# A seven-product feed-forward stage: raw weights of every other tile in slots of their own, the sums and the last block formed earlier, low parts of the down weights on VectorE

## The chip, the cores and the metric

The kernel runs on one NeuronCore of a Trainium2 chip. The metric is the device time of one execution in microseconds: 2243.45 us, the median of three runs (2242.74 to 2244.39). Five engines run their own instruction streams in order: TensorE (PE, matrix products), VectorE (DVE), ScalarE (ACT), GpSimd (POOL) and SyncE (SP, which here issues the transfers). They wait for one another only through semaphores.

## The reference

One step of a small decoder trunk, in fp32, for a prompt of 1024 + 16 tokens and 8 sample sequences of 4 tokens, model width 1024, two layers. Every layer adds a mixer (layer 0: a state-space model beside a short convolution; layer 1: a Conformer convolution module) and then a feed-forward part of hidden width 2816, 22 tiles of 128 columns:

```python
def conv_ffn(xn, fbuf, p, l):
    u = xn @ p['w_ffn_up'][l]
    a, g = jnp.split(u, [D_FF], axis=-1)
    a_c, nbuf = causal_dwconv(a, fbuf, p['w_ffn_conv'][l])
    return (jax.nn.silu(a_c) * g) @ p['w_ffn_down'][l], nbuf
```

So for each hidden tile there are two up products (a and g), a causal depthwise convolution of width 3 over a, silu, a product with g, and the down product, which is added to the residual. At the end stands a final rmsnorm.

## The kernel before

Tokens are worked on in two parts (hf = 0 and 1), and every stage runs part by part. To keep fp32 accuracy every matrix is split into a high and a low part, and a product of two matrices is three matmuls: high by high, low by high, high by low. For a weight block that means a transfer into `raw`, ScalarE's copy to the high part (`wh`) and a subtraction (`wl = raw - wh`).

The change touches the last stage alone: layer 1, tokens of part 1 (560 columns), `f1.run(1, "v", None, finals, out0)`. Its up products use a Strassen-like scheme, `up7`: the two weight blocks of a hidden tile (128x1024 each, a and g) are cut in halves a11, a12, a21, a22 of 128x512. From them come the sums s1 = a21 + a22, s2 = s1 - a11, s4 = a12 - s2 and s3 = a11 - a21, and seven products of 280 columns take the place of eight: w11, ws1, w12, ws2, ws4, ws3 and a22. Each is 12 matmuls, so a tile is 84. In between, VectorE and ScalarE move results from the accumulators (`bx`, `by`, `bz`) into `ap` and `g`, form the convolution `c` (ScalarE starts it, two VectorE operations end it), then silu into `s`, `s` times `g`, and the split of `s` into `hh` and `hl`, the operands of the down product. The a22 product is held back (`self.pend`) and issued in the next tile or in the down (`flush`); its result goes into `s` by one more VectorE operation.

The 22 tiles run in groups: f0 and f1, then four at a time (f2 to f5, ..., f18 to f21). After the up tiles of a group comes its down product, 8 output blocks of 24 matmuls for each tile of 128x1024 `w_down`; the first up tile of the next group is issued ahead of it. So f2 is issued before the down of f0 and f1, and f3 is the first up tile after it; f6 comes before the down of f2 to f5 and f7 after it, and so on with f10 and f14; the last group is issued whole ahead of the down of f14 to f17.

The order of instructions on each engine is the work of a scheduler, which moves instructions from their place in the program by its own estimates of when inputs are ready; what it makes of it is fixed when the kernel is built. The raw weights have two buffers of 4 KB per partition ("raw", `bufs=2`) in a ring: a transfer waits until the block that was there has been read by all of its users, and transfers that SP issues later wait behind it. In `up7`, a11 and a12 are the one block and a21 and a22 the other. `slot(tag, ...)` takes a slot from pools that other stages have used ("v", "xh", "t", "x"). `weight()` loads the down weights through the same ring; its low part is formed by POOL or VectorE by a counter (`WPOOL`), if no engine is given. `L1167` scales a block of the first part's final output, `L1168` sends it off; these run as fill-in work during the stage. In the changed program all lines from L869 on are some 7 higher (L870 is L877, L897 is L904, L1167 is L1174).

Of the kernel before, what the change touches and what calls it, by code (L numbers as in the profile page):

```python
# [12 lines left out]
F32 = mybir.dt.float32  # L13
F32R = mybir.dt.float32r
# [7 lines left out]
P = 128  # L22
# [15 lines left out]
FT = FF // P  # L38
# [13 lines left out]
MUL, ADD, SUB = ALU.mult, ALU.add, ALU.subtract  # L52
# [12 lines left out]
GROUPS = grp(0, 2, 2) + grp(2, FT, 4)  # L65


def build(nc, tc, ctx, a):
# [8 lines left out]
    def slot(tag, name, shape, dt=F32):  # L77
        if isinstance(shape, int):
            shape = [P, TN[shape]]
        n = math.prod(shape[1:])  # L80
        assert n <= SW
        t = sl.tile([P, SW], dt, tag=tag, name=name, bufs=COUNT[tag])
        v = t[:shape[0], :n]
        if len(shape) > 2:
            n = " ".join(f"d{i}" for i in range(len(shape) - 1))
            v = v.rearrange(f"p ({n}) -> p {n}", **{f"d{i}": shape[i + 1] for i in range(len(shape) - 2)})
        return v
# [12 lines left out]
    def tt(o, x, y, op, e=V):  # L100
        return e.tensor_tensor(o, x, y, op=op)  # L101
# [675 lines left out]
    class FFN:  # L777
        def __init__(self, layer, xs, rs, dead=0):

            self.layer, self.xs, self.rs, self.dead = layer, xs, rs, dead  # L780
            self.fw = sm.tile([P, FT, 3], F32, tag="fw", name="fw")
            SY.dma_start(self.fw, a["w_fconv"][layer])
            self.fin = sm.tile([P, FT, NS, 2], F32, tag="fin", name="fin")
            SY.dma_start(self.fin, a["ffn_in"][layer])
            self.fout = sm.tile([P, FT, NS + 1, 2], F32, tag="fout", name="fout")
            self.carry = sm.tile([P, FT, 2], F32, tag="carry", name="carry")
            self.pend = None

        def up(self, f, hf, tag, htag="t"):
            rs, fw, n = self.rs[hf], self.fw[:, f], ntok(hf)  # L790
# [32 lines left out]
        def prepare(self, xr, gi, r):  # L823


            self.ops = {n: [] for n in ("B11", "B21", "B22", "T1", "T2", "T3", "N4")}
            self.pend = None
            H = self.H = TN[1] // 2

            def hl(t, *names):  # L830
                h, l = slot("xh", "oh", 1, F32R), slot("xh", "ol", 1, F32R)
                A.activation(h, t, AF.Copy)
                tt(l, t, h.bitcast(F32), SUB)
                for i, n in enumerate(names):
                    self.ops[n].append((h[:, i * H:(i + 1) * H], l[:, i * H:(i + 1) * H]))

            for k in range(KT // 2):
                xa, xb, x2 = [slot("xh", n, 1) for n in ("xa", "xb", "x2")]
                for o, i in ((xa, k), (xb, k + KT // 2)):
                    V.scalar_tensor_tensor(o, xr[i][1], gam[:, gi, i:i + 1], r, op0=MUL, op1=MUL)  # L840
                if k % 2 == 0:
                    x4 = slot("xh", "x4", 1)
                (p, q), (b21, b22) = [(t[:, :H], t[:, H:]) for t in (xa, xb)]
                t2, t3 = x2[:, :H], x2[:, H:]
                tt(t3, b22, q, SUB)
                tt(q, q, p, SUB)
                tt(t2, b22, q, SUB)
                tt(x4[:, k % 2 * H:(k % 2 + 1) * H], b21, t2, SUB)
                hl(xa, "B11", "T1")
                hl(xb, "B21", "B22")  # L850
                hl(x2, "T2", "T3")
                if k % 2:
                    hl(x4, "N4", "N4")

        def up7(self, f, tag, htag, stag, atag):


            fw, n, H = self.fw[:, f], ntok(1), self.H
            o, M = 2 + n, P * KT // 2
            raws = []  # L860
            for i in range(2):
                raw = wp.tile([P, 1024], F32, tag="raw", name="raw", bufs=2)
                SY.dma_start(raw, a["w_up"][(self.layer * FT + f) * 2 + i])
                raws.append(raw)

            def ring():
                return [wp.tile([P, 1024], F32R, tag=t, name=t, bufs=WB) for t in ("wh", "wl")]

            def hl(hl_, raw):  # L869
                A.activation(hl_[0], raw, AF.Copy)  # L870
                tt(hl_[1], raw, hl_[0].bitcast(F32), SUB)
                return hl_

            def halves(w):
                return [[t[:, i * M:(i + 1) * M] for t in w] for i in range(2)]

            (a11, a12), (a21, a22) = [(t[:, :M], t[:, M:]) for t in raws]  # L877
            w11, w12 = halves(ring())
            hl(w11, a11)
            s1, s2, s3, s4 = [slot(stag, "s%d" % i, [P, M]) for i in range(1, 5)]  # L880
            tt(s1, a21, a22, ADD)
            ws1, ws2 = halves(ring())
            hl(ws1, s1)
            hl(w12, a12)
            tt(s2, s1, a11, SUB)
            hl(ws2, s2)
            tt(s4, a12, s2, SUB)
            ws4, ws3 = halves(ring())
            hl(ws4, s4)
            tt(s3, a11, a21, SUB)  # L890
            hl(ws3, s3)
            w22 = hl([slot(atag, "a22" + c, [P, M], F32R) for c in "hl"], a22)

            def product(b, w, x, start):
                for k, xk in enumerate(self.ops[x]):
                    for i in range(3):
                        state["pe"] = PE.matmul(  # L897
                            b[:, :H], w[i == 2][:, k * P:(k + 1) * P], xk[i == 1],
                            start=(start and k == 0 and i == 0), stop=(k == KT // 2 - 1 and i == 2),
                            skip_group_check=True)  # L900

            bx, by, bz = [bank("mm", "mm") for _ in range(3)]
            ap = slot(tag, "ap", [P, o + 6 * NS])
            PL.tensor_copy(ap[:, 0:2], self.carry[:, f])  # L904
            PL.tensor_copy(s6(ap, o)[:, :, 0:2], self.fin[:, f])
            g = slot("t", "g", [P, H])
            product(bx, w11, "B11", True)
            A.activation(ap[:, 2:2 + H], bx[:, :H], AF.Copy)
            product(by, ws1, "T1", True)
            A.activation(g, by[:, :H], AF.Copy)  # L910
            product(bz, w12, "B21", True)
            tt(ap[:, 2:2 + H], ap[:, 2:2 + H], bz[:, :H], ADD)
            product(bx, ws2, "T2", False)
            m = n - H
            sa, sp = s6(ap, o)[:, :, 2:6], ap[:, 2 + H:o]
            A.activation(sp, bx[:, :m], AF.Copy)
            A.activation(sa, sj(bx, m), AF.Copy)
            product(by, ws4, "B22", False)
            tt(sp, sp, by[:, :m], ADD)
            tt(sa, sa, sj(by, m), ADD)  # L920
            PL.tensor_copy(self.fout[:, f], last2(ap, o))
            nc_ = n + 6 * NS
            c = slot(tag, "c", [P, nc_ + 2])
            conv3(c, ap, fw, nc_)
            s = slot("t", "s", 1)
            A.activation(s[:, :n], c[:, :n], AF.Silu)
            A.activation(sj(s), s6(c, o)[:, :, 0:4], AF.Silu)
            self.flush()
            product(bx, ws3, "T3", False)
            tt(g, g, bx[:, :H], ADD)  # L930
            tick(84 * H / 2400, tt(s[:, H:], s[:, H:], g, MUL))
            h = {}

            def rest():
                product(bx, w22, "N4", False)
                tt(s[:, :H], s[:, :H], bx[:, :H], MUL)
                h[1] = split(s, "h", 1, tag=htag)

            self.pend = rest
            return h  # L940
# [6 lines left out]
        def down(self, fs, hs, hf, done, tail=None, at={}):  # L947
            cur = {}

            def tiles(m, fs, hs):  # L950
                n = len(fs)
                u, r = divmod(m * n, KT)
                i = self.layer * FT + fs[0] + u
                if i not in cur:
                    cur[i] = kept("w_down", i) if tail else \
                        weight("w_down", i, PL if at and m < 3 else V if at else None)
                return [(*(kslice if tail else wslice)(cur[i], r + i_), hs[i_]) for i_ in range(n)]

            def get(m):
                if m == 1:  # L960
                    self.flush()
                return sum([tiles(m, fs[i:i + 4], hs[i:i + 4]) for i in range(0, len(fs), 4)], [])

            if tail:
                return tail(get)
            d = self.dead if hf == 0 else 0
            residual(get, done, xres, (hf,), blk=((d, TN[0] - d),) if d else None, at=at)
# [412 lines left out]
```

## Time and profile before

| What | Value |
|---|---|
| median of three runs | 2243.45 us |
| profiled execution | 2242.73 us, of which span 2240.9 us |
| granted TensorE clock, mean | 0.990 |
| TensorE busy | 2185.1 us, 98% of the span |
| VectorE, ScalarE, POOL busy | 1694.9, 827.9, 734.3 us |
| last stage, first up tile to the end | 1821.5 to 2240.9 us |

The share of busy time hides that the stage in question consists of stretches with different limits, so it is read by stretches. Names such as f5 don't stand in the profile; which tile an operation belongs to follows from the order of the program. A line of the timeline gives the start, the duration, the engine, the line of the program, the operation and, in brackets, how long the engine was idle before and what ended that wait. L101 is the helper of all VectorE and POOL additions, subtractions and products, so the names of the tiles tell its instructions apart; L113 is ScalarE's copy in `weight()`, L870 that in `up7`; L145 is the helper of the down and other plain products, L897 the product in `up7`.

### The profile page before, as it was taken

Reading aid. Unit: us, or ns where it says so; the run is one execution under the profiler, and the core shown is the slowest. Engines: PE = TensorE matmul, PEld = TensorE weight load, DVE = VectorE, ACT = ScalarE, POOL = GpSimd, SP = SyncE. Lnnn points to the kernel's source line nnn. Section 1 sums busy time; section 2 is a strip of 40 time slices with the busy share of each in tenths; the row PEclk is TensorE's granted clock in tenths of the full one; section 3 lists DMA queues with packets and bytes.
Section 4 is the critical chain, followed back from the end, with each engine's and each line's share of the span. In section 5 each row is a group of like instructions: output and inputs, shape, how many; then the busy total and the mean of one; then the engine's idle time right before and its main releaser. Section 6 shows DMA issues by size and latency. Waiting matters only on the chain.

```text
span 2240.9 us, 34315 instructions
## 1 busy us (share of the span) xinstructions
PE 2185.1 (98%) x13504; PEld 1982.3 (88%) x13504; DVE 1694.9 (76%) x2872; ACT 827.9 (37%) x1255; POOL 734.3 (33%) x632
## 2 busy tenths in 40 slices
PE   7999999999999999999999999999999997999997
PEld 6888898888888889999999998888887987999997
DVE  8979966545544678888896789899998387878784
ACT  5122354322332423232234523333335343455452
POOL 3212114323333434333443426455454401110011
PEclk8999999999999999999999999999999999999998
DMA  5234541223222332222222353232322222333231
GB/s 170 94 97 132 187 142 50 94 94 94 94 94 94 94 94 86 85 85 85 85 77 93 94 109 99 94 94 85 112 86 87 84 76 94 113 95 95 87 105 61
DMA packets 98338, 218.07 MB, mean 97 GB/s; under 512 B 28417, under 2 KB 45185, under 8 KB 98177
## 3 DMA queue, kind: packets, MB, share of 16 engines
q1 hardware_dynamic: 97632, 215.37, 31.1%
q8 instruction: 106, 1.74, 0.3%
q10 hardware_dynamic: 544, 0.52, 0.1%
q14 instruction: 56, 0.45, 0.1%
HBM read 202.49 MB, written 13.36 MB: 96 GB/s over the span
## 4 chain that ended last, share of the span: by engine, by line
PE 76%; DVE 13%; issue 3%; DMA 3%; ACT 2%; POOL 1%; SPq 1%; POOLq 0%; ACTq 0%; DVEq 0%
PE mm L145 66%; PE mm L897 8%; DVE c L501 2%; DVE wl L101 1%; DMA raw<-w_up 1%; DVE cvb L1052 1%; DVE cva L1052 1%; DVE xr L101 1%; DMA x<-x 1%; DVE xnl L163 1%; DMA raw<-w_down 1%; DVE hl L101 1%; ACT wh L113 1%; DVE s L101 1%; PE bcs L253 1%
## 5 line engine op out<-in xcount | busy, mean ns | idle before, releaser
L101 POOL TENSOR_TENSOR wl<-raw,wh 128x1024 fp32r<-128x1024 f32 x181 | 444.2, 2454 | 662.0 <-ACT wh L113 619.9
L145 PE MATMUL mm<-xnh,wh 128*128 128x280 f32 (+3 forms) x2176 | 637.7, 337 | 6.7 <-ACT xnh L162 6.7
L145 PE MATMUL mm<-xnl,wh 128*128 128x280 f32 (+3 forms) x2176 | 641.2, 338 | 2.5 <-DVE xnl L163 2.5
L145 PE MATMUL mm<-xnh,wl 128*128 128x280 f32 (+3 forms) x2176 | 639.3, 338 | 0.0
L113 ACT ACTIVATE wh<-raw 128x1024 fp32r<-128x1024 f32 x300 | 317.5, 1058 | 662.2 <-PE mm L145 580.6
L145 PEld LDWEIGHTS mm<-xnh,wh 128*128 128x128 f32 x2176 | 376.6, 189 | 47.5 <-ACT xnh L162 6.7
L145 PEld LDWEIGHTS mm<-xnl,wh 128*128 128x128 f32 x2176 | 375.6, 188 | 46.0 <-DVE xnl L163 4.2
L145 PEld LDWEIGHTS mm<-xnh,wl 128*128 128x128 f32 x2176 | 376.9, 189 | 40.3 <-issue 0.8
L145 PE MATMUL mm<-hh,wh 128*128 128x280 f32 (+2 forms) x992 | 288.6, 329 | 13.9 <-ACT hh L159 7.1
L145 PE MATMUL mm<-hl,wh 128*128 128x280 f32 (+2 forms) x992 | 288.7, 327 | 0.0
L145 PE MATMUL mm<-hh,wl 128*128 128x280 f32 (+2 forms) x992 | 287.2, 327 | 0.3 <-POOL wl L101 0.3
L101 DVE TENSOR_TENSOR xr<-mm,xr 128x280 f32<-128x280 f32 (+4 forms) x328 | 160.5, 515 | 118.9 <-PE mm L145 118.7
L101 DVE TENSOR_TENSOR wl<-raw,wh 128x1024 fp32r<-128x1024 f32 (+1 forms) x163 | 180.3, 1116 | 28.1 <-ACT wh L113 17.5
L145 PEld LDWEIGHTS mm<-hh,wh 128*128 128x128 f32 x992 | 174.3, 189 | 30.4 <-ACT hh L159 7.3
L501 DVE SCALAR_TENSOR_TENSOR c<-ap,fw,c 128x576 f32<-128x576 f32 (+2 forms) x176 | 170.0, 966 | 27.8 <-ACT c L499 25.4
L145 PEld LDWEIGHTS mm<-hl,wh 128*128 128x128 f32 x992 | 174.5, 189 | 14.3
L145 PEld LDWEIGHTS mm<-hh,wl 128*128 128x128 f32 x992 | 173.5, 189 | 14.9 <-POOL wl L101 0.7
L1052 DVE SCALAR_TENSOR_TENSOR cva<-vp,w_dw,cva 128x512 f32<-128x512 f32 x240 | 178.9, 746 | 0.0
L1052 DVE SCALAR_TENSOR_TENSOR cvb<-vp,w_dw,cvb 128x512 f32<-128x512 f32 x240 | 178.8, 746 | 0.0
L101 POOL TENSOR_TENSOR s<-s,g 128x512 f32<-128x512 f32 (+2 forms) x66 | 92.2, 1397 | 206.7 <-DVE g L101 176.8
L897 PE MATMUL mm<-oh,wh 128*128 128x280 f32 x528 | 154.4, 294 | 5.6 <-ACT wh L870 2.7
L897 PE MATMUL mm<-ol,wh 128*128 128x280 f32 x528 | 154.3, 294 | 0.0
(264 smaller groups left out, 3119.8 us busy)
## 6 DMA issues: line engine op xcount, KB each, us to landing
raw<-w_up SPq DMA_DIRECT2D x176, 512.0 KB
raw<-w_down SPq DMA_DIRECT2D x88, 512.0 KB
raw<-w_pw SPq DMA_DIRECT2D x48, 512.0 KB
raw<-w_in SPq DMA_DIRECT2D x22, 512.0 KB
raw<-w_out SPq DMA_DIRECT2D x12, 512.0 KB
du<-up SPq DMA_DIRECT2D x8, 292.0 KB
u<-du SPq DMA_DIRECT2D x32, 73.0 KB
x<-x SPq DMA_DIRECT2D x8, 280.0 KB
```

The costliest lines, as they stand in the source:

```text
L101: return e.tensor_tensor(o, x, y, op=op)
L113: A.activation(h, raw, AF.Copy)
L145: state["pe"] = PE.matmul(banks[b][:, :n_], wl if i == 2 else wh, xx[:, t0:t0 + n_], start=(k == 0 and i == 0), stop=(k == n - 1 and i == 2))
L163: V.scalar_tensor_tensor(l, src, scale, h.bitcast(F32), op0=MUL, op1=SUB)
L253: PE.matmul(b[:, c * w:(c + 1) * w], one1[:w], dg[:, c0 + c], start=True, stop=True)
L501: mk = V.scalar_tensor_tensor(dst[:, :n], src[:, k:k + n], w[:, k:k + 1], dst[:, :n], op0=MUL, op1=ADD)
L897: state["pe"] = PE.matmul(b[:, :H], w[i == 2][:, k * P:(k + 1) * P], xk[i == 1], start=(start and k == 0 and i == 0), stop=(k == KT // 2 - ...
L1052: V.scalar_tensor_tensor(b, v, w, b, op0=MUL, op1=ADD)
```

## The change

Three edits. First, the two weight blocks of the odd tiles f1 to f17 no longer go through the ring: each half comes by a transfer of its own (four of 128x512) into slots "v", named `rw`. The even tiles and f18 to f21 keep the ring. Second, s3 is formed right behind s1, and the split of a22 comes ahead of s2 and s4 and no longer last. Third, where this stage's operands exist (`self.ops`), `weight("w_down", ...)` forms the low part on VectorE and no longer by the counter; nine of the stage's operations on POOL go to VectorE.

```diff
@@ -784,7 +784,7 @@
-            self.pend = None
+            self.ops = self.pend = None
@@ -824,7 +824,6 @@
             self.ops = {n: [] for n in ("B11", "B21", "B22", "T1", "T2", "T3", "N4")}
-            self.pend = None
@@ -859,8 +858,16 @@
             raws = []
             for i in range(2):
-                raw = wp.tile([P, 1024], F32, tag="raw", name="raw", bufs=2)
-                SY.dma_start(raw, a["w_up"][(self.layer * FT + f) * 2 + i])
+                src = a["w_up"][(self.layer * FT + f) * 2 + i]
+                if f % 2 and f < GROUPS[-1][0]:
+
+                    raw = [slot("v", "rw", [P, M]) for _ in range(2)]
+                    for j in range(2):
+                        SY.dma_start(raw[j], src[:, j * M:(j + 1) * M])
+                else:
+                    raw = wp.tile([P, 1024], F32, tag="raw", name="raw", bufs=2)
+                    SY.dma_start(raw, src)
+                    raw = [raw[:, :M], raw[:, M:]]
                 raws.append(raw)
@@ -874,22 +881,22 @@
-            (a11, a12), (a21, a22) = [(t[:, :M], t[:, M:]) for t in raws]
+            (a11, a12), (a21, a22) = raws
             w11, w12 = halves(ring())
             hl(w11, a11)
             s1, s2, s3, s4 = [slot(stag, "s%d" % i, [P, M]) for i in range(1, 5)]
             tt(s1, a21, a22, ADD)
+            tt(s3, a11, a21, SUB)
             ws1, ws2 = halves(ring())
             hl(ws1, s1)
             hl(w12, a12)
+            w22 = hl([slot(atag, "a22" + c, [P, M], F32R) for c in "hl"], a22)
             tt(s2, s1, a11, SUB)
             hl(ws2, s2)
             tt(s4, a12, s2, SUB)
             ws4, ws3 = halves(ring())
             hl(ws4, s4)
-            tt(s3, a11, a21, SUB)
             hl(ws3, s3)
-            w22 = hl([slot(atag, "a22" + c, [P, M], F32R) for c in "hl"], a22)
@@ -953,7 +960,7 @@
                     cur[i] = kept("w_down", i) if tail else \
-                        weight("w_down", i, PL if at and m < 3 else V if at else None)
+                        weight("w_down", i, PL if at and m < 3 else V if at or self.ops else None)
```

Three places show how the instructions moved. The first is VectorE around the end of f8 and the start of f9 (f9 is the last tile of its group; f13 and f17 have the same pattern, f5 nearly). Before, where s1_18800, s2_18801, s3_18802 and s4_18803 are those of f9, c_18624, g_18555 and s_18628 are f7's, and 186xx else is f8:

```order
L101 TENSOR_TENSOR ap_18552<-ap_18552,mm_18550 128x8x4
L101 TENSOR_TENSOR s1_18800<-raw_18794 128x512
L501 SCALAR_TENSOR_TENSOR c_18624<-ap_18552,fw_13586,c_18624 128x576
L101 TENSOR_TENSOR s2_18801<-s1_18800,raw_18792 128x512
L501 SCALAR_TENSOR_TENSOR c_18624<-ap_18552,fw_13586,c_18624 128x576
L101 TENSOR_TENSOR g_18555<-g_18555,mm_18549 128x280
L101 TENSOR_TENSOR wl_18669<-s4_18656,wh_18668 128x512
L101 TENSOR_TENSOR wl_18669<-s3_18655,wh_18668 128x512
L101 TENSOR_TENSOR s4_18803<-raw_18792,s2_18801 128x512
L101 TENSOR_TENSOR s_18628<-s_18628,g_18555 128x280
L101 TENSOR_TENSOR ap_18682<-ap_18682,mm_18681 128x280
L101 TENSOR_TENSOR s3_18802<-raw_18792,raw_18794 128x512
```

Now, where c_18770, g_18701, s_18774 and mm_18695 are f8's, and s1_18820 to s4_18823 and rw are f9's:

```order
L101 TENSOR_TENSOR wl_18817<-rw_18808,wh_18816 128x512
L101 TENSOR_TENSOR wl_18817<-rw_18809,wh_18816 128x512
L101 TENSOR_TENSOR s_18774<-s_18774,mm_18695 128x280
L101 TENSOR_TENSOR s_18774<-s_18774,g_18701 128x280
L101 TENSOR_TENSOR s1_18820<-rw_18812,rw_18813 128x512
L101 TENSOR_TENSOR s3_18822<-rw_18808,rw_18812 128x512
L101 TENSOR_TENSOR hl_18791<-s_18644,hh_18790 128x560
L101 TENSOR_TENSOR a22l_18833<-rw_18813,a22h_18832 128x512
L101 TENSOR_TENSOR s2_18821<-s1_18820,rw_18808 128x512
L101 TENSOR_TENSOR wl_18827<-s1_18820,wh_18826 128x512
L101 TENSOR_TENSOR wl_18841<-s3_18822,wh_18840 128x512
L101 TENSOR_TENSOR s4_18823<-rw_18809,s2_18821 128x512
```

The sums of f9 stood among the operations of f7; now they stand behind the two last operations on s of f8, the first of which takes the result of f8's a22 product (mm_18695).

The second is TensorE at the same place. Before, where wh_18668 is ws3 and ws4 of f8, a22 is f7's, and wh_18796 and wh_18805 are w11 and ws1 of f9:

```order
L897 MATMUL mm_18680<-oh_16814,wh_18668 128x280
L897 MATMUL mm_18680<-ol_16815,wh_18668 128x280
L897 MATMUL mm_18680<-oh_16814,wl_18669 128x280
L897 MATMUL mm_18549<-oh_16822,a22h_18545 128x280
L897 MATMUL mm_18549<-ol_16823,a22h_18545 128x280
L897 MATMUL mm_18549<-oh_16822,a22l_18546 128x280
L897 MATMUL mm_18826<-oh_16742,wh_18796 128x280
L897 MATMUL mm_18826<-ol_16743,wh_18796 128x280
L897 MATMUL mm_18827<-oh_16742,wh_18805 128x280
L897 MATMUL mm_18827<-ol_16743,wh_18805 128x280
L897 MATMUL mm_18826<-oh_16742,wl_18797 128x280
```

Now, where a22 is f8's and wh_18816 is w11 of f9:

```order
L904 MATMUL mm_18695<-oh_16822,a22h_18681 128x280
L904 MATMUL mm_18695<-ol_16823,a22h_18681 128x280
L904 MATMUL mm_18695<-oh_16822,a22l_18682 128x280
L904 MATMUL mm_18846<-oh_16742,wh_18816 128x280
L904 MATMUL mm_18846<-ol_16743,wh_18816 128x280
L904 MATMUL mm_18846<-oh_16742,wl_18817 128x280
L904 MATMUL mm_18846<-oh_16763,wh_18816 128x280
L904 MATMUL mm_18846<-ol_16764,wh_18816 128x280
L904 MATMUL mm_18846<-oh_16763,wl_18817 128x280
```

The first product of f9 was mixed into the products of f8; now it begins when the last matmul of f8's a22 has been issued.

The third is ScalarE ahead of the first down, before (wh_17673 is f3's, raw_17597 is the second down tile, c_17461 and s_17465 are f2's):

```order
L159 ACTIVATE hh_17314<-s_17168 128x560
L113 ACTIVATE wh_17599<-raw_17597 128x1024
L870 ACTIVATE a22h_17382<-raw_17354 128x512
L910 ACTIVATE g_17392<-mm_17387 128x280
L870 ACTIVATE wh_17673<-raw_17669 128x512 x2
L499 ACTIVATE c_17461<-ap_17389,fw_13586 128x576
L926 ACTIVATE s_17465<-c_17461 128x528
L927 ACTIVATE s_17465<-c_17461 128x32
L159 ACTIVATE hh_17481<-s_17298 128x560
```

and now (wh_17681 is f3's, raw_17601 the second down tile, c_17465 and s_17469 are f2's):

```order
L877 ACTIVATE a22h_17376<-raw_17358 128x512
L113 ACTIVATE wh_17603<-raw_17601 128x1024
L917 ACTIVATE g_17396<-mm_17391 128x280
L499 ACTIVATE c_17465<-ap_17393,fw_13586 128x576
L877 ACTIVATE wh_17681<-rw_17673 128x512
L933 ACTIVATE s_17469<-c_17465 128x528
L934 ACTIVATE s_17469<-c_17465 128x32
L159 ACTIVATE hh_17485<-s_17302 128x560
L877 ACTIVATE wh_17681<-rw_17674 128x512
```

The a22 split of f2 passed the copy of the second down tile, and c of f2 passed the copies of f3's first block, the second of which now comes behind hh.

## The prediction

> **What bounds the kernel now.** I read the waits of TensorE first, then the engines by stretch of the last stage, then the chain and the timelines at the largest wait. Waits of TensorE from 1805 us on (total, times, longest):
>
> ```profile
> PE mm L145 <- ACT hh L159: 7.1, 1, 7.1
> ...
> PE mm L897 <- ACT wh L870: 2.7, 2, 2.0
> PE mm L897 <- ACT ap L917: 2.5, 2, 2.1
> PE mm L145 <- DVE xr L101: 1.7, 1, 1.7
> PE mm L145 <- DVE s L101: 1.6, 1, 1.6
> ```
>
> The stage by stretches: width, then PE, PEld, DVE, ACT, POOL busy with counts, granted clock, DMA share, GB/s.
>
> ```profile
> 1821.50:1889.50 68.00, 53.52 (x367) 51.63 (x366) 54.23 (x103) 26.23 (x54) 9.86 (x12) 0.90 0.29 93
> 1889.50:1940.00 50.50, 48.81 (x374) 48.16 (x373) 40.84 (x77) 27.23 (x56) 6.74 (x13) 1.00 0.34 115
> 1940.00:2155.00 215.00, 215.00 (x1670) 215.00 (x1669) 172.30 (x323) 107.14 (x213) 21.86 (x44) 1.00 0.29 91
> 2155.00:2180.00 25.00, 24.01 (x184) 23.55 (x183) 19.05 (x36) 13.35 (x27) 4.80 (x6) 1.00 0.36 115
> ```
>
> The third row decides the case. For 215 us, from the down of f2 to f5 to the last group, TensorE never stops: 1670 matmuls at 215.00/1670 = 0.1287 us. There nothing can be won, and what comes a microsecond late costs a microsecond. At that pitch the first row's 367 matmuls need 47.2 of 68 us and the second's 374 need 48.1 of 50.5. So earlier weights can bring at most 20.8 + 2.4 us in f0 to f5, and 1.0 in the fourth row (25.00 less 24.01).
>
> **The start, f0 to f2 and the first down.** The chain that ended last (start, us, what), then the engines beside it:
>
> ```profile
> 1851.27 3.52 DMA raw<-w_down
> ...
> 1857.24 3.59 DMA raw<-w_down
> ...
> 1860.91 1.06 ACT wh L113
> ...
> 1865.06 3.51 DMA raw<-w_up
> ...
> 1880.23 9.24 PE mm L145 x66
> 1889.47 4.65 PE mm L897 x36
> ```
>
> ```profile
> 1862.52 2.51 DVE L101 TENSOR_TENSOR a22l<-raw,a22h 128x512 fp32r<-128x512 f32 x1 [1.29 <-ACT a22h L870]
> ...
> 1875.78 1.72 DVE L1167 SCALAR_TENSOR_TENSOR xr<-xr,gam,rstd 128x496 f32<-128x496 f32 x1
> 1877.42 1.78 DVE L101 TENSOR_TENSOR hl<-s,hh 128x560 fp32r<-128x560 f32 x1
> ```
>
> ```profile
> 1868.67 1.15 ACT L870 ACTIVATE wh<-raw 128x512 fp32r<-128x512 f32 x2 [5.89 <-DMA raw<-w_up]
> 1869.72 0.76 ACT L499 ACTIVATE c<-ap,fw 128x576 f32<-128x576 f32 x1
> 1873.32 0.64 ACT L926 ACTIVATE s<-c 128x528 f32<-128x528 f32 x1 [2.84 <-DVE c L501]
> 1873.87 0.21 ACT L927 ACTIVATE s<-c 128x32 f32<-128x32 f32 x1
> 1873.99 0.65 ACT L159 ACTIVATE hh<-s 128x560 fp32r<-128x560 f32 x1
> ```
>
> ```profile
> 1862.10 2.38 POOL L101 TENSOR_TENSOR wl<-raw,wh 128x1024 fp32r<-128x1024 f32 x1 [11.40 <-ACT wh L113]
> ...
> 1875.19 3.42 POOL L101 TENSOR_TENSOR xr<-xr,rstd 128x496 f32<-128x496 f32 x2 [8.86 <-ACT rstd L264]
> ```
>
> The wait of 7.05 us ends at 1874.70. Before it, f3's weights were requested only at 1865.06, when a22l of f2 had freed the ring; they landed at 1868.57; and c of f2, which the down waits for, stood on ScalarE behind the two wh of f3. In the changed order wl of the second down tile is on VectorE: ScalarE's wh ends at 1861.97, wl takes 1.2 us, so the ring transfer ahead of f3's four (f4's second half) is issued at about 1863.2 and f3's first block at 1863.6. A block of 128x1024 takes 3.5 us to land; half of one, with another block ahead, I put at 3 to 3.7: landed by 1866.6 to 1867.3. c of f2 now stands ahead of wh of f3, so what is left is one wh (0.6), s (0.8) and hh (0.6): the down restarts near 1868.9, 5.8 us earlier. Not all of it lasts. Before f3's products the accumulators must be emptied (second wait, 1.65 us, to 1880.23), and VectorE now has s1, s3 and a wl of f3 (0.6 each), the xr of L1167 (now L1174), s2, one hl and a22l ahead of that, while POOL's two xr (3.42 us) still slow the middle of it by about a microsecond each, as 1.72 and 1.78 show. From 1868.9 with 0.35 + 0.35 + 0.65 + 3 x 0.6 + 1.7 + 0.6 + 0.7 to 1.7 + 0.6: restart at 1875.6 to 1876.6, say 1876.0; plus the same 9.24 us, f3 starts at 1885.2 and not 1889.47: **-4.2**. The waits of 2.0 and 2.1 us inside f0 to f2 may go too, but f3's start hangs on the two w_down transfers in the chain (3.52 and 3.59), which keep their place. Bounds: nothing, to the 20.8 us that are lost there; the walk itself allows -1 to -8.
>
> **f3 to f5's cover and the wait of 1.58 us before the next down**: with f3 prefetched and the POOL parts on VectorE, I find no late product there, so **-2.4** (bounds 0 and -2.4).
>
> **The odd tiles inside the groups.** f3, f7, f11 and f15 are formed during a down, in both orders. f5, f9, f13 and f17 are not, and there the order is worse than it was. Before, VectorE formed s1, s2, s4 and s3 of f9 between the pieces of f7 and f8, and TensorE mixed f9's first products into f8's ws3 and a22. Now s1 of f9 stands behind the product of s with f8's a22 block, and TensorE's first product of f9 behind all of f8's a22. Durations, from the middle stretch and its timeline:
>
> ```profile
> L101 DVE TENSOR_TENSOR wl<-s,wh 128x512 fp32r<-128x512 f32 x56 | 36.1, 683 | 0.9 <-ACT wh L870 0.8
> ...
> L101 DVE TENSOR_TENSOR a22l<-raw,a22h 128x512 fp32r<-128x512 f32 x14 | 9.6, 684 | 0.3
> ...
> L101 DVE TENSOR_TENSOR g<-g,mm 128x280 f32<-128x280 f32 x13 | 5.7, 440 | 0.2
> ...
> L101 DVE TENSOR_TENSOR wl<-raw,wh 128x1024 fp32r<-128x1024 f32 x4 | 4.9, 1226 | 1.1 <-ACT wh L113 0.9
> ```
>
> ```profile
> L870 ACT ACTIVATE wh<-s 128x512 fp32r<-128x512 f32 x56 | 32.4, 625 | 46.2 <-issue 15.2 <-PE mm L897 13.2 <-PE mm L145 12.2
> ...
> L908 ACT ACTIVATE ap<-mm 128x280 f32<-128x280 f32 x14 | 5.6, 398 | 2.3 <-PE mm L897 1.8
> ```
>
> ```profile
> 2052.81 0.73 DVE L101 TENSOR_TENSOR hl<-s,hh 128x560 fp32r<-128x560 f32 x1
> 2053.46 0.68 DVE L101 TENSOR_TENSOR s<-s,raw 128x512 f32<-128x512 f32 x1
> ...
> 2056.83 1.29 DVE L101 TENSOR_TENSOR wl<-s,wh 128x512 fp32r<-128x512 f32 x2
> 2058.03 0.50 DVE L101 TENSOR_TENSOR ap<-ap,mm 128x248 f32<-128x248 f32 x2
> 2058.46 0.43 DVE L101 TENSOR_TENSOR s<-s,mm 128x280 f32<-128x280 f32 x1
> 2058.81 0.68 DVE L101 TENSOR_TENSOR a22l<-raw,a22h 128x512 fp32r<-128x512 f32 x1
> ```
>
> From start to start a 128x512 on VectorE costs 0.60 us, hl 0.65, a 128x280 0.35. Count from the end of f8's a22, with 0.2 until VectorE sees it (my estimate). VectorE: two s 0.9, s1 1.5, s3 2.1, hl 2.8, a22l 3.4, s2 4.0, wl of s1 4.6, wl of s3 5.2, s4 5.8, s1 and s3 of f10 7.0, ap 7.3, wl of s2 7.9, a22l of f10 8.5, wl of s4 9.1. TensorE: w11 to 1.54; ws1 needs wh of s1, which is ready at 2.75 (s1, then ScalarE's ap and wh): 1.2 late. Two matmuls, w12 to 4.55, wl of s1 just in time, ten matmuls and two of ws2 to 6.1; then two of f10, whose wh stands behind wh of s4 and is ready at 7.0: 0.9 late. Then wl of s2 at 8.0: 0.45 late. The 62 matmuls that take 8.0 us end at 10.6. With the 0.75 that a22 itself waits for g of f8 (0.44 and its signals), since nothing stands between ws3 and a22 any more, that is 3.4 us. **f9, f13, f17: 3 x 3.4 = +10.2.** At f5 L1174 (0.64) and s1, s3 and a22l of f6 stand ahead too: wl of s1 at 7.05, and TensorE loses 1.4 + 2.35 + 1.05 + 0.75 = 5.5. After its wait of 2.0 us TensorE also ran slowly, here in the first row, and still more after the 7.05:
>
> ```profile
> 1825.20:1829.50 4.30, 4.28 (x22) 4.28 (x23) 4.30 (x9) 1.86 (x3) 0.00 (x0) 0.64 0.15 19
> ...
> 1874.70:1877.50 2.80, 2.80 (x12) 2.80 (x13) 2.80 (x5) 1.60 (x3) 2.31 (x2) 0.50 0.53 170
> ```
>
> 22 matmuls need 2.83 us at the usual pitch and took 4.3. I add half of that 1.4 for the wait of 2.35: **f5: +6.2.** Bounds for a late tile: 0.75 (only g's wait) to 5.5 (as at f5). The Trainium skill ("TensorE: Matmul & The Clock Gate", What's actually happening) has the clock halve after an idle window of about 3.4 us; by that the wait of 2.35 us need not slow anything, and the sum would be 0.7 less. The granted 0.64 after 2.03 us speaks against taking it as a threshold.
>
> **wl of nine down tiles** goes from POOL to VectorE: 9 x 1.14 = 10.3 us more there, during downs, where VectorE has 43 us free in 215; a wl that was off the path stays so. I take 0, bounds -1 and +3. If that cover is gone, each costs up to 1.2. The Trainium skill ("SBUF — State Buffer", SBUF: two separate sides) says a VectorE operation with two SBUF inputs and a GpSimd operation that reads SBUF lock each other out for the whole instruction. By it the move would free VectorE nine times of up to 1.8 us (2.51 less 0.68), 16 us in all. The trace agrees at the first of the nine, at 1862.52; a22l's mean of 684 ns in the middle stretch, where five of them ran, shows nothing of it. f18 to f21 stay as they are: 0.
>
> **Sum**: 2242.7 (the profiled execution, 0.7 below the median of 2243.45) - 4.2 - 2.4 + 6.2 + 10.2 = **2252.5 us**.
>
> **Rivals.** *The waits of the start go and the odd tiles cost little* (faster): VectorE and ScalarE reach f9's parts earlier than I count, because c, g and s of f8 are short and 43 us are free in the stretch. It decides once a late tile costs under 1.5 us. At 1 us each, with -8 and -2.4 at the start: 2242.7 - 10.4 + 4 = 2236. For it speaks the size of the 7.05 us; against it that s1 waits for a22's end whatever VectorE did before. *They cancel* (same): -6, -2.4 and 4 x 2.2 give 2243. *The transfers are late as well*: on SP's queue f9's four stand behind both of f10, which wait for f8's ring blocks. The cover is an estimate: f8's blocks come free some 8 us into f7, f9's then land some 6 us later (3.5 us, and the data of f10 ahead), and they are wanted at the end of f8, 2 x 84 x 0.1287 = 21.6 us after f7's start. Were it gone and they 3 us late at each of the four tiles, 2252.5 + 12 = 2264. So raw blocks that "arrive early" would arrive later than now. *Only the start changes back and forth* (the change does not do what it says): f3's blocks, issued behind f4's, land no sooner than before, 0 in place of -4.2, and 2256.7.
>
> **Numbers.** My forecast with its nearer variants (2248 to 2261) 0.70, late transfers 0.06, cancelling 0.15, faster 0.09. Within 0.2% (4.5 us) of the median is what a measurement cannot tell from no change: 2239 to 2248. So faster 0.09, same 0.15, slower 0.76. The range from 2243.5 to 2261 takes in the forecast and the upper half of the cancelling case; it leaves out the faster rival, the late transfers and the lower half.
>
> **What would show it.** TensorE waits for VectorE's wl and ScalarE's wh (now L877) three or four times at each of f5, f9, f13 and f17, where there are none now; a stretch as long in matmuls as the 215 us has some 10 us idle; s1<-rw stands on VectorE right after s<-s,mm. f3's first product begins 9.24 us after a restart near 1876. The forecast is wrong if these tiles run without a gap, or if f3 starts more than 10 us earlier.

## The result, and the profile after

The changed kernel takes 2261.1 us (median of 4 runs, 2258.78 to 2264.01); the kernel before, beside it on the same chip, 2243.09 us (4 runs, 2241.76 to 2244.39). The ratio is 1.0078, with a 95% interval of 1.0063 to 1.0093: slower, by some 17 to 18 us, where 9.8 were forecast. The time lies at the very end of the range, 8.6 us above the 2252.5 that were forecast.

The profiled execution has a span of 2259.9 us and not 2240.9. Waits of TensorE from 1805 us on, changed kernel (total, times, longest):

```profile
PE mm L904 <- ACT wh L877: 9.5, 10, 2.0
PE mm L145 <- DVE s L101: 6.6, 4, 3.5
PE mm L904 <- DVE g L101: 4.5, 5, 1.2
...
PE mm L145 <- DVE xr L101: 4.2, 1, 4.2
PE mm L904 <- DVE wl L101: 2.3, 2, 2.1
PE mm L904 <- ACT g L917: 1.9, 4, 1.0
```

The 7.05 us for hh are gone. In their place stand many short waits in `up7` (L904), for wh, g and wl, and longer ones in the down. The same stretches as before, as times from the start of the trace:

```profile
1821.50:1889.50 68.00, 54.73 (x375) 52.70 (x374) 56.68 (x110) 28.26 (x56) 5.40 (x13) 0.90 0.28 95
1889.50:1940.00 50.50, 45.76 (x338) 44.74 (x337) 39.23 (x70) 26.18 (x53) 1.84 (x12) 0.97 0.30 101
1940.00:2155.00 215.00, 204.20 (x1550) 200.14 (x1549) 161.76 (x297) 97.28 (x193) 9.82 (x33) 1.00 0.26 84
```

The first stretch got 8 matmuls more done than before (375 and 367). The second got 36 fewer, and the third, in which TensorE never stopped before, 120 fewer: at 0.1287 us each 15.4 us. Only 10.8 of them (215.00 less 204.20) show as idle time. A row inside the stretch, TensorE at ws1 of f9, shows where the rest is:

```profile
1990.66 0.29 PE L904 MATMUL mm<-oh,wl 128*128 128x280 f32 x1
1991.96 0.40 PE L904 MATMUL mm<-oh,wh 128*128 128x280 f32 x1 [1.01 <-ACT wh L877]
1992.20 0.29 PE L904 MATMUL mm<-ol,wh 128*128 128x280 f32 x1
```

From 1990.66 to 1992.20 two matmuls took 1.54 us in place of 0.26, a loss of 1.28 for a wait that is shown as 1.01: the matmuls before it are drawn 0.29 long but follow one another at 0.13, and the first after a wait takes 0.24 until the next starts. Each wait thus costs 0.27 more than is shown, and with 15 waits in the stretch that is 4.1 us: 10.8 + 4.1 = 14.9 of the 15.4.

Where the time came from can be read off TensorE's first product of f3, f7, f11 and f15, with which `up7` goes on behind each down. The first line is the first matmul of the whole stage. Before:

```profile
1821.49 0.29 PE L897 MATMUL mm<-oh,wh 128*128 128x280 f32 x1
...
1889.31 0.29 PE L897 MATMUL mm<-oh,wh 128*128 128x280 f32 x1
...
1959.88 0.29 PE L897 MATMUL mm<-oh,wh 128*128 128x280 f32 x1
...
2027.82 0.29 PE L897 MATMUL mm<-oh,wh 128*128 128x280 f32 x1
...
2095.95 0.29 PE L897 MATMUL mm<-oh,wh 128*128 128x280 f32 x1
```

And now, the same five:

```profile
1823.46 0.29 PE L904 MATMUL mm<-oh,wh 128*128 128x280 f32 x1
...
1889.47 0.29 PE L904 MATMUL mm<-oh,wh 128*128 128x280 f32 x1
...
1966.61 0.29 PE L904 MATMUL mm<-oh,wh 128*128 128x280 f32 x1
...
2039.55 0.29 PE L904 MATMUL mm<-oh,wh 128*128 128x280 f32 x1
...
2112.45 0.29 PE L904 MATMUL mm<-oh,wh 128*128 128x280 f32 x1
```

The stage itself begins 1.97 us later in this execution. The change touches nothing ahead of it, and in the other runs it begins anywhere from 1821.00 to 1823.67, so this is no effect of the change, and times are counted from the stage's first matmul here. From there f3 begins 1.8 us earlier than before (66.0 for 67.8), f7 4.8 us later, f11 9.8, f15 14.5, and the end (by the spans) comes 17.0 later. So 1.8 us are won up to f3, 6.6 are lost from f3 to f7, then 5.0 and 4.8 in the two groups behind, and 2.5 from f15 to the end, where the third late tile, f17, lies.

VectorE at the end of f8 in the changed kernel:

```profile
1984.95 0.51 DVE L101 TENSOR_TENSOR ap<-ap,mm 128x248 f32<-128x248 f32 x2 [3.70 <-PE mm L904]
...
1988.18 1.29 DVE L101 TENSOR_TENSOR wl<-rw,wh 128x512 fp32r<-128x512 f32 x2
1989.52 0.45 DVE L101 TENSOR_TENSOR s<-s,mm 128x280 f32<-128x280 f32 x1
1989.89 0.44 DVE L101 TENSOR_TENSOR s<-s,g 128x280 f32<-128x280 f32 x1
1990.25 1.29 DVE L101 TENSOR_TENSOR s<-rw 128x512 f32<-128x512 f32 x2
```

s<-rw (s1 and s3 of f9) starts when a22's result is in s, as the order has it. VectorE had been idle for 3.70 us just before 1984.95. The transfers were not what it waited for. SP's queue shows when they were issued; the DMA rate from 1965 to 1995, in slices of 0.75 us, shows when the data had come:

```profile
1973.73 1.80 SPq L866 DMA_DIRECT2D rw<-w_up  x4
```

```profile
GB/s 295 213 0 0 0 0 0 0 0 22 0 0 126 224 391 350 366 361 276 5 0 0 0 0 0 0 0 0 0 0 0 0 0 0 0 0 0 22 0 0
```

By 1980 the data had landed, ten microseconds ahead of s1.

### The profile page after: what moved, and what is told of

It is laid out like the page before. It is cut to its first block, busy times and chain, and to the rows that moved or that the text cites. A ratio compares the mean times of both kernels' runs of the same rounds, so it can differ in the third digit from the quotient of the medians.

```text
span 2259.9 us, 34354 instructions
## 1 busy us (share of the span) xinstructions
PE 2190.1 (97%) x13504; PEld 1983.6 (88%) x13504; DVE 1703.3 (75%) x2881; ACT 828.9 (37%) x1255; POOL 710.7 (31%) x623
## 4 chain that ended last, share of the span: by engine, by line
PE 75%; DVE 14%; issue 3%; DMA 3%; ACT 2%; POOL 1%; SPq 1%; POOLq 0%; DVEq 0%; ACTq 0%
PE mm L145 65%; PE mm L904 7%; DVE c L501 2%; DVE wl L101 2%; DVE s L101 1%; DVE cvb L1059 1%; DMA rw<-w_up 1%; DVE cva L1059 1%; DVE xr L101 1%; DVE xnl L163 1%; DVE hl L101 1%; ACT wh L113 1%; PE bcs L253 1%; DVE cv L101 1%; SPq L737 1%
## 5 line engine op out<-in xcount | busy, mean ns | idle before, releaser
L101 POOL TENSOR_TENSOR wl<-raw,wh 128x1024 fp32r<-128x1024 f32 x172 | 422.3, 2455 | 599.3 <-ACT wh L113 578.5
L904 PE MATMUL mm<-oh,wh 128*128 128x280 f32 x528 | 156.1, 297 | 11.4 <-ACT wh L877 9.5
L904 PE MATMUL mm<-oh,wl 128*128 128x280 f32 x528 | 152.3, 296 | 2.5 <-DVE wl L101 2.3
```

The costliest lines, as they stand in the source:

```text
L904: state["pe"] = PE.matmul(b[:, :H], w[i == 2][:, k * P:(k + 1) * P], xk[i == 1], start=(start and k == 0 and i == 0), stop=(k == KT // 2 - ...
```

## The experiments

Theory A: the slots of the odd tiles make the order that forms f5, f9, f13 and f17 late, and this order is the loss. Theory B: the early s3 and a22, or the low parts on VectorE, put too much ahead of what is wanted. Theory C: the small transfers or the slots cost time wherever they are. All edits are against the changed kernel, unless it is said otherwise. Ratios are to the kernel before, run on the same chip.

| Experiment | us | ratio | 95% interval |
|---|---|---|---|
| the change | 2261.1 | 1.0078 | 1.0063 to 1.0093 |
| only the slots | 2257.6 | 1.0058 | 1.0043 to 1.0073 |
| only s3 and a22 early | 2243.8 | 0.9994 | 0.9984 to 1.0003 |
| only the low parts on VectorE | 2241.2 | 0.9983 | 0.9974 to 0.9993 |
| all but the slots | 2241.4 | 0.9986 | 0.9977 to 0.9995 |
| slots, transfers earlier in the program | 2246.9 | 1.0011 | 1.0002 to 1.0020 |
| slots for f1, f3, f7, f11, f15 | 2248.2 | 1.0018 | 1.0008 to 1.0027 |
| slots for f1, f3 | 2244.1 | 0.9996 | 0.9987 to 1.0005 |
| slots for f3 | 2242.8 | 0.9995 | 0.9985 to 1.0004 |
| slots for f5, f9, f13, f17 | 2254.1 | 1.0048 | 1.0035 to 1.0062 |
| POOL's two xr on VectorE | 2260.8 | 1.0075 | 1.0059 to 1.0090 |
| what helped, alone | 2239.8 | 0.9982 | 0.9973 to 0.9991 |
| the same, POOL's two xr on VectorE | 2237.5 | 0.9972 | 0.9960 to 0.9983 |

### Only the slots

The kernel before with the first edit alone; s3 and the a22 split stand last, as they did, and the low parts go by the counter.

> Only the first edit: the odd tiles' blocks in slots of their own; s3 and a22 at their old places in the program, low parts of the down weights by the counter as before. Theory A (the slots make the order that forms f5, f9, f13 and f17 late): the order still shows s1 of these tiles behind the a22 result of the tile before, so TensorE waits 3 to 4 us at each of f9, f13, f17 and more at f5, and the time is 2255 to 2263. Theory B (the earlier s3 and a22, or the nine low parts on VectorE, put too much ahead of what is wanted): the late tiles cost little here and the time is 2236 to 2247.

The ratio of 1.0058 is theory A's. VectorE forms s1 of f9 (1986.41) behind the result of a22 (1985.69) here too, and the first two waits at f9 are there, 0.69 for g and 1.01 for wh of s1 (0.68 and 1.01 in the changed kernel); the late tile doesn't come from the sequence in the program. The smaller waits at f9 (0.58 and 0.29) are not there; in their place TensorE waits 1.60 and 1.07 us in the next down.

### Only the new sequence, only the low parts on VectorE, and both

The second edit alone, against the kernel before:

```diff
             tt(s1, a21, a22, ADD)
+            tt(s3, a11, a21, SUB)
...
             hl(w12, a12)
+            w22 = hl([slot(atag, "a22" + c, [P, M], F32R) for c in "hl"], a22)
...
-            tt(s3, a11, a21, SUB)
             hl(ws3, s3)
-            w22 = hl([slot(atag, "a22" + c, [P, M], F32R) for c in "hl"], a22)
```

> Only the second edit: s3 behind s1 and the a22 split ahead of s2 and s4, all blocks through the ring. Theory A: s1 of f9 stands ahead of f8's a22 again, no wait of more than 1 us at f9, f13, f17, and the wait of 7 us at the first down stays: 2239 to 2248. Theory B: VectorE has two more operations ahead of s2, f9, f13 and f17 each lose 1 to 3 us, 2247 to 2254.

The third edit alone, against the kernel before:

```diff
-            self.pend = None
+            self.ops = self.pend = None
...
-                        weight("w_down", i, PL if at and m < 3 else V if at else None)
+                        weight("w_down", i, PL if at and m < 3 else V if at or self.ops else None)
```

> Only the third edit: nine low parts of down weights on VectorE. Theory A: they lie in the downs, where VectorE has time; the a22l beside the first one takes 0.7 and not 2.5 us, which brings the blocks of f3 about 1.8 us earlier: 2239 to 2244. Theory B: 10 us more on VectorE show as waits of TensorE in the downs, 2245 to 2254.

Both, that is the changed kernel without its slots:

```diff
-                src = a["w_up"][(self.layer * FT + f) * 2 + i]
-                if f % 2 and f < GROUPS[-1][0]:
...
+                raw = wp.tile([P, 1024], F32, tag="raw", name="raw", bufs=2)
+                SY.dma_start(raw, a["w_up"][(self.layer * FT + f) * 2 + i])
                 raws.append(raw)
```

> The second and third edits together, all blocks through the ring: the changed kernel without its slots. Theory A: without the slots nothing is formed late, 2236 to 2246, and some 17 us less than the changed kernel's 2261. Theory B: most of the loss of 18 us stays, 2252 to 2261.

The new sequence alone can't be told from no change (the wait of 7.05 us, which was to stay, is 5.87 there), the low parts on VectorE win a little (0.9983), both together as much (0.9986). Theory B falls as the account of the loss; the slots cost some 20 us (1.0078 less 0.9986, of 2244 us). Alone they cost 13 (1.0058), so the three edits don't simply add up: alone they come to 8 us, together to 17.5. Why the slots cost more with the other two edits, no run takes apart. The run with both has TensorE's first waits of the first down and one wait ahead of a later down as follows:

```profile
1869.74 1.41 PE L145 MATMUL mm<-hh,wh 128*128 128x280 f32 x5 [3.76 <-ACT hh L159]
...
1874.13 0.84 PE L145 MATMUL mm<-hl,wh 128*128 128x280 f32 x2 [2.28 <-DVE hl L101]
```

```profile
2007.32 0.40 PE L145 MATMUL mm<-hh,wh 128*128 128x280 f32 x1 [1.21 <-DVE s L101]
```

So the start is won without any slot: the wait of 7.05 us is down to 3.76, and the down resumes at 1869.74, ahead of the 1871.41 of the changed kernel. From the stage's first matmul, f3 begins 4.2 us earlier than before (63.7 for 67.8), where the changed kernel won 1.8. The row at 2007.32 is what the new sequence costs from f4 on, a wait ahead of the downs that the kernel before had once, at 1939.66, and not in its middle stretch; the run with the sequence alone has the same 1.21 us, at 2008.10 and 2077.67.

### The slots, with the transfers placed earlier in the program

```diff
-                if f % 2 and f < GROUPS[-1][0]:
...
+            if f % 2 and f < GROUPS[-1][0]:
+                raws = self.early
+            else:
+                if f < GROUPS[-1][0]:
+                    self.early = rw(f + 1)
```

Here `rw(f)` takes the four slots and issues their four transfers.

> The changed kernel with all nine odd tiles in their slots, but the four transfers of an odd tile are placed in the program ahead of the two ring blocks of the even tile before it, so that on SP's queue they no longer stand behind the ring blocks of a later tile. Theory A (what costs is that the scheduler takes the blocks to be late and puts their forming behind the a22 result of the tile before): s1 of f5, f9, f13 and f17 stands ahead of that result again, the waits of 0.7 + 1.0 us go, and the time is 2238 to 2248. Theory C (256 KB transfers into slots, or the slots themselves, cost the time wherever they are issued): 2254 to 2262.

With a ratio of 1.0011, of the loss of 17 to 18 us two to three are left, with all nine tiles still in slots. VectorE forms s1 and s3 of f9 (1975.87) ahead of the a22 result of f8's forerunner f7 (s<-s,mm at 1981.63) and long ahead of f8's own:

```profile
1975.87 1.28 DVE L101 TENSOR_TENSOR s<-rw 128x512 f32<-128x512 f32 x2
...
1981.63 0.44 DVE L101 TENSOR_TENSOR s<-s,mm 128x280 f32<-128x280 f32 x1
```

What was expected of SP's queue did not come: f9's four transfers still stand there behind four ring blocks, as they do in the changed kernel.

```profile
1937.08 32.23 SPq L876 DMA_DIRECT2D raw<-w_up  x4
1969.36 1.85 SPq L864 DMA_DIRECT2D rw<-w_up  x4
```

The same place on the queue, the same small transfers, and no late tile: theory C falls for the main part, and so does the thought that the queue made them late. It is the order in which the scheduler forms them. TensorE waits nowhere at f9 here; what is left are waits of 1.6 us ahead of the downs (2012.02, 2081.88). Why the scheduler forms the odd tiles late when their transfers are written behind the even tile's, no run shows.

### Slots for some of the tiles

```diff
-                if f % 2 and f < GROUPS[-1][0]:
+                if f in (1, 3, 7, 11, 15):
```

> The changed kernel with slots only for f1, f3, f7, f11 and f15 (f1 and the first up tiles after a down); f5, f9, f13 and f17 through the ring. Theory A: f5 to f17 lose nothing, f1 still stalls: 2238 to 2246. Theory C: five of nine tiles in slots keep about half of the loss, 2249 to 2255.

The same line with `(1, 3)`:

> The changed kernel with slots only for f1 and f3. Theory A: what is gained at the start by f3 stays and nothing is lost later: 2236 to 2244. Theory C: two of nine tiles in slots keep about 4 us, 2244 to 2249.

With `f == 3`:

> The changed kernel with slots for f3 alone. Theory A: as with f1 and f3, without f1's wait for its late sums, but f1 is followed by a start that hangs on the transfers of the down tiles anyway: 2235 to 2243. Were f1's late sums what costs at the start, this run is 3 us or more ahead of the one with both.

With `(5, 9, 13, 17)`:

> The changed kernel with slots only for f5, f9, f13 and f17, the last tiles of their groups; f1, f3, f7, f11 and f15 through the ring. Theory A (the late forming of these four is the loss): 2255 to 2262, waits of 0.7 for g, 1.0 for wh and 0.6 for wh at each of f9, f13 and f17 as in the changed kernel. Theory C (the loss is spread over all nine slotted tiles): about half of it, 2247 to 2253.

Against the run without slots (0.9986), f5, f9, f13 and f17 cost 0.0062 or 14 us, the other five 0.0032 or 7 us, together 21, and all nine 0.0092 or 20.6. The two sets simply add up. So theory A holds for two thirds of the loss: the last run came out just under its 2255, and the first of the four missed both forecasts. Of its 7 us, f1 and f3 may cost about 2 (0.9996 less 0.9986, whose intervals overlap; the 2244.1 us of the run with both lie where its two forecasts meet); the other 5 (1.0018 less 0.9996) fall to f7, f11 and f15, which are formed in the down. The prediction had them free, and they are not. The third stretch, 1940 to 2155, of the runs without slots, with the five, and with the four:

```profile
1940.00:2155.00 215.00, 212.48 (x1644) 211.81 (x1643) 174.34 (x324) 104.33 (x210) 11.77 (x39) 1.00 0.30 91
```

```profile
1940.00:2155.00 215.00, 209.59 (x1613) 208.25 (x1614) 170.79 (x317) 101.17 (x204) 10.19 (x36) 1.00 0.27 84
```

```profile
1940.00:2155.00 215.00, 207.30 (x1579) 203.89 (x1578) 167.07 (x308) 99.21 (x196) 11.30 (x36) 1.00 0.26 87
```

The kernel before does 1670 matmuls there. What the five lose is waits in the down: TensorE's, in the same stretch of that run (the run without slots has 2.4 us there, the two waits of 1.21):

```profile
PE mm L145 <- ACT hh L159: 2.8, 2, 1.4
PE mm L145 <- DVE xr L101: 1.9, 2, 1.3
PE mm L145 <- DVE hl L101: 0.7, 1, 0.7
```

In its order s1, s3, a22l and s2 of the tile after the down stand on VectorE beside hl and the emptying of the accumulators, for which the down waits. The changed kernel shows the same at f11, where s1 and s3 wait for the slots' transfers besides, and the down's s stands behind them; TensorE goes on at 2020.90 after 0.70 us for it:

```profile
2017.99 1.29 DVE L101 TENSOR_TENSOR s<-rw 128x512 f32<-128x512 f32 x2 [0.99 <-DMA rw<-w_up]
...
2020.41 0.44 DVE L101 TENSOR_TENSOR s<-s,mm 128x280 f32<-128x280 f32 x1
```

The profiled executions, by TensorE's first product of f3, f7, f11 and f15 as above (us from one to the next):

| Run | stage start to f3 | to f7 | to f11 | to f15 | to the end |
|---|---|---|---|---|---|
| before | 67.8 | 70.6 | 67.9 | 68.1 | 145.0 |
| the change | 66.0 | 77.1 | 72.9 | 72.9 | 147.5 |
| all but the slots | 63.7 | 70.7 | 69.5 | 69.6 | 143.0 |
| slots for f1, f3, f7, f11, f15 | 66.1 | 72.3 | 70.1 | 70.8 | 144.5 |
| slots for f5, f9, f13, f17 | 63.1 | 75.1 | 71.9 | 72.0 | 148.2 |

With f5, f9, f13 and f17 alone the start is as good as without slots, a group costs 4 us more than before, and the waits at f9 are those of the changed kernel (0.68, 1.01, 0.57, 0.29). With the other five the start is as poor as in the changed kernel.

f3's slots bring nothing (0.9995 with them, 0.9986 without), and f1's sums cost no 3 us: the difference of the runs with and without f1 is 0.0001.

### What slows the second wait of the first down

In the changed kernel the first wait there fell from 7.05 to 3.54, and the second rose from 1.65 to 4.24. VectorE there, changed kernel, s1 and s3 of f3 and a wl, beside POOL's two xr:

```profile
1872.28 2.34 DVE L101 TENSOR_TENSOR s<-rw 128x512 f32<-128x512 f32 x2
1874.55 1.72 DVE L101 TENSOR_TENSOR wl<-rw,wh 128x512 fp32r<-128x512 f32 x1
```

The edit:

```diff
-            tt(x, x, r, MUL, PL)
+            tt(x, x, r, MUL, PL if hf else V)
```

> The changed kernel with the two xr blocks of the first part's final output that POOL scales during the first down (3.4 us) on VectorE instead. Theory D (the second wait there, 4.2 us for xr in place of 1.65, is VectorE being slowed by POOL): no VectorE operation takes over 1 us between 1868 and 1880, the second wait shrinks to 2 us or less, f3 starts 2 to 3 us earlier and the time is 2257 to 2260. Theory E (the wait is the number of operations of f3 that stand ahead of the emptying of the accumulators on VectorE, and f3's blocks that land late): the wait stays above 3 us and the time stays at 2260 to 2263.

The same two lines, and TensorE's second wait:

```profile
1872.39 1.29 DVE L101 TENSOR_TENSOR s<-rw 128x512 f32<-128x512 f32 x2
1873.60 0.68 DVE L101 TENSOR_TENSOR wl<-rw,wh 128x512 fp32r<-128x512 f32 x1
```

```profile
1877.20 0.60 PE L145 MATMUL mm<-hh,wh 128*128 128x280 f32 x1 [2.32 <-DVE xr L101]
```

Theory D has the cause of the slow operations: without POOL they take their usual time and the wait drops from 4.24 to 2.32, near the 2 us that were asked. But f3 starts 1.0 us earlier (1888.52 for 1889.47, the stage's start within 0.1), not 2 to 3, and the time stayed at 2260.8, as theory E had it. Behind its 2.32 us TensorE ran at a granted clock of 0.50 for 4 us and of 0.74 for 4 more; in the changed kernel it was 0.52 and then 1.00. At f5 the waits for wh and wl are 4.7 us where they were 3.5, with xr operations on VectorE beside its late sums, and the wait ahead of the next down is 0.54 where it was 1.65. By the traces 1.0 us is left at the end, which the times of the runs can't tell from nothing.

### What helped, alone

Without slots, with the new sequence for f0 to f3 alone and the low parts on VectorE for the first down alone, against the kernel before:

```diff
+            new = f < 4
+            if new:
+                tt(s3, a11, a21, SUB)
...
+            if new:
+                w22 = hl([slot(atag, "a22" + c, [P, M], F32R) for c in "hl"], a22)
...
-                        weight("w_down", i, PL if at and m < 3 else V if at else None)
+                        weight("w_down", i, PL if at and m < 3 else V if at or (self.ops and fs[0] == 0) else None)
```

> What helped, alone: all blocks through the ring; s3 and a22 early for f0 to f3 only, the old sequence from f4 on; the low parts of the down weights on VectorE for the first down only. Theory A: the start is that of the second and third edits together (first wait 3.8 in place of 7.05), and from f4 on there are none of the 1.2 us waits ahead of the downs that the early sequence brought: 2237 to 2242, 0.1 to 0.3% below the kernel before.

And the same with POOL's two xr on VectorE, as above:

> The run before with the two xr blocks that POOL scales during the first down on VectorE. Theory D: hl and the sums there take 0.7 and not 1.4 to 1.8 us, the second wait (2.3 us) shrinks by 1 to 2 us: 2236 to 2241. Theory E: the same as the run before within 1 us.

Both beat the kernel before, by 0.18% and 0.28%; the second is 2237.5 us. Its first two waits in the first down, against 3.75 and 2.16 in the run without the last edit:

```profile
1867.04 1.53 PE L145 MATMUL mm<-hh,wh 128*128 128x280 f32 x5 [3.82 <-ACT hh L159]
...
1869.46 0.83 PE L145 MATMUL mm<-hl,wh 128*128 128x280 f32 x2 [0.19 <-DVE hl L101]
```

2 us of wait less, and this time the whole time is 2.3 us less by the medians, though the intervals of the two overlap; by the traces f3 starts 3.1 us earlier, and 1.8 are left at the end. That the gain lasts because the tiles behind have no late sums for the two operations to delay is likely, but not shown.

## Why the prediction was right, and where its sizes were off

**The main step held.** The late sums of f9, f13 and f17 were read from the order, and TensorE's waits there came where they were counted: 0.68 for g (0.75 predicted), 1.01 for wh of s1 (1.2), 0.58 for wh of f10 (0.9). The wait of 0.45 for wl of s2 did not appear; instead there are 0.29 for g on ScalarE. With 0.27 for each of the four that is 3.6, near the 3.4. The run with slots for f5, f9, f13 and f17 alone puts the price of such a tile at 4.0 (71.9 and 72.0 for 67.9 and 68.1).

**The groups cost more: 3.4 predicted, 5.0 and 4.8 measured.** The missing part is the wait of 0.70 in the down, with its 0.27. It stands behind s1 to s2 of f11 on VectorE (the rows at 2017.99 and 2020.41); the prediction took the slots of f7, f11 and f15 to be free, and with slots for f5, f9, f13 and f17 alone this wait is not there.

**f5 and the wait of 1.58: +6.2 and -2.4, together +3.8, measured +6.6.** The waits at f5 were 1.20, 1.32 and 2.13, 4.65 in all (5.5 predicted). TensorE's clock behind the longest:

```profile
1919.80:1923.80 4.00, 3.86 (x17) 3.52 (x18) 3.51 (x7) 1.76 (x5) 0.00 (x0) 0.59 0.36 122
...
1948.00:1952.00 4.00, 3.99 (x31) 3.99 (x32) 4.00 (x8) 0.67 (x1) 0.00 (x0) 1.00 0.01 2
```

17 matmuls in 4.0 us, where 31 is usual: 1.8 us, not half of 1.4. Three times 0.27 come on top, which makes 7.3 for f5, 0.7 more than the whole interval lost. The term was about right, and the step that failed is the -2.4: the wait ahead of the next down did not go, it is 1.65 at 1948.01. In the run with slots for f5, f9, f13 and f17 alone it is gone, and f3 to f7 lose 4.5 there (75.1 for 70.6), near the 3.8. What the two runs differ in is the slots of the other five tiles, which were taken to be free; how they bring this wait back is not shown.

**The start: -4.2, measured -1.8.** The transfers went as the prediction had them. On SP's queue the second w_down and f3's four blocks stand at

```profile
1859.39 0.33 SPq L110 DMA_DIRECT2D raw<-w_down  x1
...
1865.47 1.81 SPq L866 DMA_DIRECT2D rw<-w_up  x4
```

From the stage's first matmul that is 35.9 and 42.0; before, w_down stood at 35.8, and for f3 42.1 was predicted. The down resumed 0.5 us later than predicted (1871.41, that is 47.95 for 47.41), f3's first block having taken 4.07 us to land and not 3 to 3.7. The second wait ended 1.2 us later than predicted (1879.18, 55.7 for 54.5). And the step that failed is "the same 9.24 us" from there to f3: it took 10.29 us, since TensorE ran slowly behind a wait of 4.24 us, as it had not behind the 1.65 of before. The clock in the 4 us behind each, before and now:

```profile
1880.20:1884.20 4.00, 3.97 (x30) 3.98 (x31) 3.12 (x8) 0.12 (x1) 0.00 (x0) 1.00 0.82 225
```

```profile
1879.10:1883.10 4.00, 3.92 (x17) 3.92 (x18) 4.00 (x10) 0.00 (x0) 0.00 (x0) 0.52 0.04 12
```

The prediction counted a slow clock at f5 and not here. That the gain of the first wait would be given back at the second in part was right, and that POOL slows VectorE there is shown by the runs with xr on VectorE. The -4.2 is nearly what the runs without the slots of f1 and f3 win (67.8 less 63.7 or 63.1).

**The low parts on VectorE: 0, bounds -1 and +3, measured -0.17%** (0.9983) for this edit alone, that is 3.8 us less, with an interval of 1.6 to 5.8: outside the bounds. In its profiled execution the first two waits of the first down are 6.43 and 0.96 where they were 7.05 and 1.65; where the rest lies it doesn't show.

**The rivals.** Faster, and cancelling, fell with the first: a late tile costs 4 us. "Late transfers" (2264) came nearer to the time than the forecast, but its cause is not at the late tiles: at f9 the data lay there ten microseconds early. Transfers that came late do stand ahead of the wait in the down, at f11 (0.99 us) and f15 (0.94 us).

The cause was right. That the time lies inside the range is luck in part: the start, the wait that was to go and the groups were all off to the same side, 7 us in all, and little more would have left it.

## What to carry to other kernels

An edit that only moves where data are loaded can change the order in which a scheduler forms everything that depends on them; look at that order first, on the full engine and on those that feed it, before the wait that the edit removes. In a stretch where the bounding engine never stops, more buffers have nothing to win and their side effects come in full; here the gain lay in a start of a few tiles, and to apply the other two edits there alone, without the slots, kept it. A wait that is removed at one gate can be given back at the next: find what stands behind it on the other engines, and take that away too. When two traces are compared by their times, count from the first instruction of the stage that was changed: the 2 us by which this stage began later are as large as what was won up to f3.

## What the runs showed of the hardware

A short wait of TensorE cost about 0.27 us more than its idle time says, from the rows at 1990.66 to 1992.20 (0.25 to 0.28 at all 15 waits of the middle stretch), and there this explains 4.1 us. The granted clock in the 4 us behind a wait was 0.52 after 4.24 us, 0.59 after 2.13 and 1.00 after 1.65 (the rows above). VectorE's subtraction of 128x512 took 1.72 us beside POOL's xr, and 0.68 with POOL's share on VectorE. The Trainium skill ("SBUF — State Buffer", SBUF: two separate sides) has VectorE operations with two SBUF inputs and GpSimd operations that read SBUF lock each other out; this pair of runs agrees with it.
